# Out projection of a hybrid layer: residual loaded in place, first norm spread over the second half, four gate heads ahead, down inputs staged in residual tiles

## The chip, the cores and the metric

One core of one Trainium2 chip. The metric is the device time of one execution in microseconds. A program is timed in several runs, and their median counts; one further execution is recorded by the profiler, and its instructions are the trace.

## The reference, cut to what matters

One layer of a streaming encoder: a mixer made of two branches, a projection back to the residual stream, and a SwiGLU feed-forward network, for 1024 tokens of width 1024 in float32 (16 meta tokens stand in front and are cut off at the end).

```python
merged = jnp.sum(gates * br, axis=2)          # both branches, gated
h = h + merged @ w_out                        # out projection and residual
u = rmsnorm(h, ffn_norm_w)
gt, up = jnp.split(u @ w_gate_up, 2, axis=-1) # D_FF = 2816 each
h = h + (jax.nn.silu(gt) * up) @ w_down
return rmsnorm(h, final_norm_w)[:, N_META:]
```

The change touches the part from `merged @ w_out` to the first products of the down projection.

## The kernel before, in words

**Layout.** Activations lie transposed: 128 channels on the partitions, tokens along the free axis. Width 1024 is eight tiles (KD = 8), and the 1024 tokens fall into two halves of 512 columns, h1 and h2. Every float32 product is made of three matmuls: weights and activations are split into a rounded part (`hi`, a cast on ACT) and the remainder (`lo`, a subtraction on DVE), and hi·hi, hi·lo and lo·hi are added up in PSUM. `load_w` (L130) does this for a weight block: a load on SP into `wraw` (two buffers), the cast to `whi` on ACT (L134), the subtraction to `wlo` on DVE (L135). `split` (L145) does it for activations: cast L146, subtraction L150, or L99 where GpSimd (POOL) does it.

**Out projection (L1019 to L1067).** For each half and each of eight tiles m: load the residual slice of the input into `xr` (L1024, pool `wk`, two buffers), load the weight block, 24 matmuls, one DVE instruction that scales, adds `xr` and writes `h[m]` (L1028), a store of it to DRAM for later use (L1029), and the square summed over m (`sumsq`, L939: a square on ACT, L942 or L945, and an addition on DVE, L946). After the eighth tile `total` (L948) adds over the partitions with a matmul of ones and makes the reciprocal root: three instructions, of which the reciprocal on DVE is L186. The `wk` tiles share their addresses with the tile `part` of the stage before.

**Norm and the sums for the fast product.** Gate and up are computed together by a Strassen-like scheme: 7 products of half size per pair of blocks instead of 8. Its seven activation operands are Y11, Y21 (h1 normed), t1, t2, t3, t4 (differences) and Y22 (h2 normed). After the first half the eight tiles are normed (L1032) and split into Y11 and Y21, at once, with the subtractions in turn on DVE and POOL. After the second half two `head`s (L1002: the two products of gate block j that need only Y11 and Y21, 24 matmuls) are issued for j = 0 and 1, then 8 norms, 8 differences on DVE (L1052, L1056), 8 on POOL (L1059 for t3, L1064 for t4) and 20 splits follow. The order on each engine is made by a scheduler at build time: of what is ready by its own estimate, an engine takes what stands first in the program; on the chip each engine then works through its list in that order.

**FFN loop (L1084 to L1118).** 22 pairs j. Each needs two weight loads, weight sums on POOL (`comb`, L1081, pool `w2`, opened only after `wk` is closed), their splits (`parts`, L982 on ACT and L983 on DVE, into slots of a ring), and 84 matmuls in seven products of 12, or 60 where the head is done. The result c goes to DRAM (L1118). c and two work tiles live in `res`, a pool of 11 tiles of 128x1024; eight of these hold `h` until its last use.

**Down projection (L1121 to the end).** `h` is loaded again from DRAM into eight tiles of `res` (L1124), then for six groups of up to four c: load c into `cr` (L1134, three buffers of a pool of its own), split, 2 products per tile m, added to `h[m]` on DVE (L1144). The last group also does the squares, the final norm in three column ranges and the output.

Of the kernel before, what the change touches and what calls it, by code (L numbers as in the profile page):

```python
# [20 lines left out]
NT = 1024  # L21
# [71 lines left out]
def body(tc, A):  # L93
# [863 lines left out]
    def half(blk_, k0):  # L957
        return blk_[0][:, k0:k0 + 4], blk_[1][:, k0:k0 + 4]
# [6 lines left out]
    def bank():  # L965
        banks.append(banks.pop(0))
        return psm2(banks[-1])
# [1 line left out]
    def psm2(tag):  # L969
        return psp.tile([128, 512], F32, name="pq_" + tag, tag=tag, bufs=2 if tag in ("p", "psd") else 1)  # L970

    ring = ["whi", "wlo"]

    def slot():

        ring.append(ring.pop(0))
        t = wp.tile([128, 2, 4, 128], F32R, name="ws_" + ring[-1], tag=ring[-1], bufs=2)
        return t[:, 0], t[:, 1]

    def parts(src, w):  # L980

# [30 lines left out]
        act.activation(c[:, 0:512], ps, AF.Silu)  # L1012
        return c

    f0 = None
    a0 = a
    wkp = tc.tile_pool(name="wk", bufs=2)
    wk = wkp.__enter__()
    for hf in range(2):  # L1019
        cs = slice(512 * hf, 512 * hf + 512)  # L1020
        sm = wk.tile([128, 512], F32, name="sm")
        for m in range(KD):
            x = wk.tile([128, 512], F32, name="xr")
            sp.dma_start(x, A["hT"][:, m, NM + 512 * hf:NM + 512 * hf + 512])  # L1024
            w = load_w(A["w_out"][m])
            ps = bank()
            dense(ps, w, KD, lambda k: a[hf][0][:, k], lambda k: a[hf][1][:, k], 512)
            dve.scalar_tensor_tensor(h[m][:, cs], ps, 0.5, x, op0=ALU.mult, op1=ALU.add)  # L1028
            sp.dma_start(h_dram[:, m, cs], h[m][:, cs])  # L1029
            sumsq(wk, sm, m, cs)  # L1030
        rs = total(wk, sm, 512)
        norm = lambda k: dve.scalar_tensor_tensor(h[k][:, cs], h[k][:, cs], ffnw[:, k:k + 1], rs,  # L1032
                                                  op0=ALU.mult, op1=ALU.mult)
        fb = block(KD, 512)
        if hf == 0:
            Y["11"], Y["21"] = half(fb, 0), half(fb, 4)
            for k in range(KD):
                norm(k)
                split(fb[0][:, k], fb[1][:, k], h[k][:, cs], None if k % 2 else dve)
            continue  # L1040
        for j in range(2):
            ahead[j] = head(j)
        Y["t3"], Y["22"] = half(fb, 0), half(fb, 4)
        Y["t1"], Y["t2"], Y["t4"] = (both(room16()) for _ in range(3))
        h1, h2 = slice(0, 512), slice(512, NT)

        def put(name, k, src, eng):
            split(Y[name][0][:, k], Y[name][1][:, k], src, eng)

        for k in range(4):  # L1050
            norm(k)
            dve.tensor_tensor(h[k][:, h1], h[k][:, h2], h[k][:, h1], op=ALU.subtract)  # L1052
            put("t1", k, h[k][:, h1], dve)
        for k in range(4):
            norm(k + 4)
            dve.tensor_tensor(h[k][:, h1], h[k + 4][:, h2], h[k][:, h1], op=ALU.subtract)  # L1056
            put("t2", k, h[k][:, h1], dve)
        for k in range(4):
            pool.tensor_tensor(h[k][:, h2], h[k + 4][:, h2], h[k][:, h2], op=ALU.subtract)  # L1059
            put("t3", k, h[k][:, h2], dve)  # L1060
        for k in range(4):
            put("22", k, h[k + 4][:, h2], dve)
        for k in range(4):
# [5 lines left out]
    w2p = tc.tile_pool(name="w2", bufs=2)  # L1069
    w2 = w2p.__enter__()  # L1070
    ring[:] = ["whi", "wlo", "wr"]

    def slot3():
        ring.append(ring.pop(0))
        t = (w2 if ring[-1] == "wr" else wp).tile([128, 2, 4, 128], F32R, name="ws_" + ring[-1], tag=ring[-1],
                                                  bufs=2)
        return t[:, 0], t[:, 1]

    def comb(x, y, op):
        t = w2.tile([128, 4, 128], F32, name="sw", bufs=3)  # L1080
        pool.tensor_tensor(t, x, y, op=op)  # L1081
        return t

    for j in range(FF):  # L1084
        g = raw_w(A["w_gu"][2 * j], 0)
        u = raw_w(A["w_gu"][2 * j + 1], 1)
        x11, x12, x21, x22 = g[:, 0:4], g[:, 4:8], u[:, 0:4], u[:, 4:8]
        pc = bank()
        s1 = comb(x21, x22, ALU.add)
        if j in ahead:  # L1090
            c = ahead.pop(j)
            product(pc, parts(s1, slot3()), Y["t1"], True, True)
        else:
            c = wide()
            pa = bank()
            product(pa, parts(x11, slot3()), Y["11"], True, True)
            act.copy(c[:, 512:NT], pa)
            product(pc, parts(s1, slot3()), Y["t1"], True, True)
            product(pa, parts(x12, slot3()), Y["21"], False, True)
# [5 lines left out]
        product(pb, parts(s2, slot3()), Y["t2"], True, True)  # L1105
# [3 lines left out]
        product(pd, parts(comb(x11, x21, ALU.subtract), slot3()), Y["t3"], True, True)  # L1109
        dve.tensor_tensor(v1, u4, pd, op=ALU.add)  # L1110
        pe3 = bank()
        product(pe3, parts(comb(x12, s2, ALU.subtract), slot3()), Y["22"], True, True)
        dve.tensor_tensor(c[:, 512:NT], u4, pe3, op=ALU.add)
        act.activation(c[:, 512:NT], c[:, 512:NT], AF.Silu)
        product(pd, parts(x22, slot3()), Y["t4"], False, True)
# [3 lines left out]
    w2p.__exit__(None, None, None)  # L1119

    wk = st.enter_context(tc.tile_pool(name="wk2", bufs=2))  # L1121
    h[:] = [wide() for _ in range(KD)]
    for m in range(KD):
        sp.dma_start(h[m], h_dram[:, m])  # L1124
    for n, (q0, q1) in enumerate(DOWN):
        nq = q1 - q0
        if n % 2:
# [18 lines left out]
        if q1 < FF:  # L1146
            for m in range(KD):
                w = load_w(A["w_dn"][m, :, q0:q1], nq)
                for hf in range(2):
                    down(m, w, slice(512 * hf, 512 * hf + 512))  # L1150
        else:
            room = blk.tile([128, 2, KD, 4, 128], F32R, name="wl", tag="blk")
            ws = [load_w(A["w_dn"][m, :, q0:q1], nq, (room[:, 0, m], room[:, 1, m])) for m in range(KD)]
            for cs in (slice(0, 512), slice(512, 768), slice(768, 1024)):
                sm = wk.tile([128, 512], F32, name="sm")
                for m in range(KD):
                    down(m, ws[m], cs)
                    sumsq(wk, sm, m, cs)
                c = cs.stop - cs.start
                rs = total(wk, sm, c)  # L1160
                for k in range(KD):
                    x = h[k][:, cs]
                    if c == 512:
                        dve.scalar_tensor_tensor(x, x, finw[:, k:k + 1], rs, op0=ALU.mult, op1=ALU.mult)
                    else:
                        act.activation(x, x, AF.Copy, scale=finw[:, k:k + 1])
                        (pool if k % 3 == 1 else dve).tensor_tensor(x, x, rs, op=ALU.mult)
                    (sp, act)[k // 2 % 2].dma_start(A["out"][:, k, cs], x)
# [69 lines left out]
```

## Time and profile before

| | us |
|---|---|
| median of 3 runs | 3034.86 |
| lowest and highest run | 3029.31, 3038.34 |
| the profiled execution's own time | 3037.91 |
| its span, first to last instruction | 3036.1 |

The span is the time from the first to the last instruction of the trace. In the trace each instruction has its engine, its line, its tiles and its start and duration; matmuls are pipelined, so their durations overlap, and the spacing of their starts tells their speed. A row "A <- B" in the views of waits says that A's engine stood idle until B had ended. The granted clock of TensorE (PEclk) is given as a share of full speed.

### The profile page before, as it was taken

The page shows a single profiled execution, that of the slowest core. Times are in us where ns is not written, and L with a number is a line of the kernel's source. Part 1 is how long each engine was busy: PE and PEld are TensorE (multiplying, and loading weights), DVE is VectorE, ACT ScalarE, POOL GpSimd, SP SyncE. Part 2 cuts the span into 40 slices and gives each one's busy share as a digit, 9 for nine tenths or more (in the row PEclk, how much of TensorE's full clock was granted, in tenths as well). Part 3 has the DMA queues.
Part 4 walks back from the last instruction along what each step waited for, and adds up shares of the span by engine and source line. Part 5 has one row for each costly group of instructions (what it writes and reads, how often), then busy time and mean ns, then how long its engine had stood idle before and what let it go on. Part 6 is the DMA issues. An engine that isn't in the chain of part 4 may idle for free.

```text
span 3036.1 us, 43138 instructions
## 1 busy us (share of the span) xinstructions
PE 2921.1 (96%) x16130; PEld 2452.9 (81%) x16130; DVE 1978.2 (65%) x3846; ACT 1324.8 (44%) x3319; POOL 310.0 (10%) x286
## 2 busy tenths in 40 slices
PE   7899999999999999999999999999985999998997
PEld 6788788888888889878888778888874888886886
DVE  8577687886867854767777652564767555555446
ACT  5546465556455444645555443222233333333213
POOL 2200000000000000000010100000102333330000
PEclk9999999998999999999999999999997999999998
DMA  3121111110211211111111124352342222226312
GB/s 104 42 58 38 46 50 41 52 57 22 64 42 36 76 47 47 36 63 43 46 53 41 65 72 158 104 173 91 111 153 90 98 83 84 84 84 204 91 56 80
DMA packets 118889, 226.27 MB, mean 75 GB/s; under 512 B 46952, under 2 KB 53768, under 8 KB 118680
## 3 DMA queue, kind: packets, MB, share of 16 engines
q1 hardware_dynamic: 116952, 221.42, 22.3%
q8 instruction: 127, 2.08, 0.3%
q10 hardware_dynamic: 1728, 2.10, 0.2%
q14 instruction: 82, 0.67, 0.1%
HBM read 174.09 MB, written 49.38 MB: 74 GB/s over the span
## 4 chain that ended last, share of the span: by engine, by line
PE 83%; DVE 10%; ACT 3%; issue 2%; DMA 1%; POOL 1%; SPq 0%; DVEq 0%; ACTq 0%; POOLq 0%
PE psd L142 14%; PE psd L143 14%; PE psd L141 14%; PE pq_psd L993 1%; PE pq_p L995 1%; PE pq_psd L995 1%; PE pq_psd L994 1%; PE pq_p L993 1%; PE pq_p L994 1%; PE ps_p L561 1%; PE ps_o L639 1%; PE ps_o L746 1%; PE ps_a L617 1%; PE ps_a L629 1%; PE ps_o L619 1%
## 5 line engine op out<-in xcount | busy, mean ns | idle before, releaser
L142 PE MATMUL psd<-u_lo,whi 128*128 128x512 f32 (+3 forms) x2136 | 770.2, 361 | 3.7 <-DVE u_lo L150 2.3
L141 PE MATMUL psd<-u_hi,whi 128*128 128x512 f32 (+3 forms) x2136 | 763.8, 358 | 1.6 <-ACT raw L374 1.6
L143 PE MATMUL psd<-u_hi,wlo 128*128 128x512 f32 (+3 forms) x2136 | 757.1, 355 | 4.1 <-DVE wlo L135 4.1
L134 ACT CAST whi<-wraw 128x1024 fp32r<-128x1024 f32 (+2 forms) x197 | 188.1, 955 | 652.7 <-PE psd L142 467.7
L142 PEld LDWEIGHTS psd<-u_lo,whi 128*128 128x128 f32 x2136 | 408.4, 191 | 42.0 <-issue 6.8
L143 PEld LDWEIGHTS psd<-u_hi,wlo 128*128 128x128 f32 x2136 | 405.2, 190 | 37.2 <-DVE wlo L135 4.7
L141 PEld LDWEIGHTS psd<-u_hi,whi 128*128 128x128 f32 x2136 | 404.1, 189 | 38.0 <-issue 4.0
L135 DVE TENSOR_TENSOR wlo<-wraw,whi 128x1024 fp32r<-128x1024 f32 (+2 forms) x197 | 217.9, 1106 | 158.0 <-ACT whi L134 148.2
L143 PE MATMUL psd<-blk,wlo 128*128 128x512 f32 x512 | 199.4, 390 | 0.9 <-DVE wlo L135 0.9
L141 PE MATMUL psd<-blk,whi 128*128 128x512 f32 x512 | 199.2, 389 | 0.0
L142 PE MATMUL psd<-blk,whi 128*128 128x512 f32 x512 | 199.2, 389 | 0.0
L374 ACT COPY raw<-psd 128x256 f32<-128x256 f32 x165 | 73.4, 445 | 92.5 <-PE psd L143 89.0
L143 PEld LDWEIGHTS psd<-blk,wlo 128*128 128x128 f32 x512 | 96.1, 188 | 21.6 <-DVE wlo L135 1.8
L906 DVE TENSOR_TENSOR part<-part,psd 128x512 f32<-128x512 f32 x96 | 65.7, 684 | 72.7 <-PE psd L143 72.5
L141 PEld LDWEIGHTS psd<-blk,whi 128*128 128x128 f32 x512 | 96.1, 188 | 20.1
L142 PEld LDWEIGHTS psd<-blk,whi 128*128 128x128 f32 x512 | 96.1, 188 | 19.9
L700 DVE TENSOR_TENSOR xdt<-ps_z,dtb 128x512 f32<-128x512 f32 (+1 forms) x36 | 24.8, 690 | 105.3 <-PE ps_z L697 105.3
L1081 POOL TENSOR_TENSOR sw<-wraw 128x512 f32<-128x512 f32 x44 | 67.1, 1526 | 255.9 <-DMA wraw<-w_gu 244.8
L539 DVE TENSOR_TENSOR X<-X,itmp 66x30 f32<-66x30 f32 (+14 forms) x240 | 85.9, 358 | 5.2
L99 POOL TENSOR_TENSOR qk<-raw,qk 128x400 f32<-128x400 f32 x16 | 30.5, 1908 | 537.3 <-ACT raw L380 423.6
L537 DVE TENSOR_TENSOR itmp<-X 66x30 f32<-66x30 f32 (+14 forms) x240 | 80.8, 337 | 5.5
L421 ACT ACTIVATE Es<-ps_p,cum 128x128 f32<-128x128 f32 x256 | 75.5, 372 | 11.0 <-PE ps_p L418 10.9
(689 smaller groups left out, 6307.6 us busy)
## 6 DMA issues: line engine op xcount, KB each, us to landing
wraw<-w_in SPq DMA_DIRECT2D x105, 512.0 KB, 3.4
wraw<-w_gu SPq DMA_DIRECT2D x46, 512.0 KB, 3.4
wraw<-w_br SPq DMA_DIRECT2D x36, 512.0 KB, 3.4
c<-hc SPq DMA_DIRECT2D x22, 512.0 KB, 2.6
cr<-c SPq DMA_DIRECT2D x22, 512.0 KB, 4.1
wraw<-w_dn SPq DMA_DIRECT2D x40, 256.0 KB, 2.7
g<-zt SPq DMA_DIRECT2D x32, 256.0 KB, 2.0
y_d<-zt SPq DMA_DIRECT2D x32, 256.0 KB, 2.0
```

Of the source, the lines that this page charges most:

```text
L134: act.copy(hi[:, 0:kk], raw[:, 0:kk])
L135: dve.tensor_tensor(lo[:, 0:kk], raw[:, 0:kk], hi[:, 0:kk], op=ALU.subtract)
L141: pe.matmul(ps[:, 0:n], hi[:, wk0 + k], ahi(k), start=(k == 0), stop=False)
L142: pe.matmul(ps[:, 0:n], hi[:, wk0 + k], alo(k), start=False, stop=False)
L143: pe.matmul(ps[:, 0:n], lo[:, wk0 + k], ahi(k), start=False, stop=(k == kk - 1))
L374: dense_u((name, lambda ps, p0, p1: act.copy(raw[:, 3 + p0:3 + p1], ps)))
L421: act.activation(E[0:L, i, 0:L], ps[0:L, 128 * i:128 * i + L], AF.Relu, bias=cum[0:L, c, h0 + h:h0 + h + 1], scale=-1.0)
L537: dve.tensor_tensor(t, X[:, 0:j, j:j + 1].broadcast_to([66, j, m]), X[:, j:j + 1, j + 1:32].broadcast_to([66, j, m]), op=ALU.mult)
L539: dve.tensor_tensor(X[:, 0:j, j + 1:32], X[:, 0:j, j + 1:32], t, op=ALU.add)
L906: dve.tensor_tensor(part[:, m, cs], part[:, m, cs], ps, op=ALU.add)
L993: pe.matmul(ps, w[0][:, k], y[0][:, k], start=start and k == 0, stop=False, skip_group_check=not start)
L1081: pool.tensor_tensor(t, x, y, op=op)
```

## The change

What it does:

1. The residual slice is loaded straight into `h[m]`, and the scaled sum is added in place; the `xr` buffers go. The first half's sum of squares lies in a `res` tile.
2. The norm and the split of first-half tile m-1 are issued behind second-half tile m, one tile at a time, all on DVE.
3. Four heads (j = 0 to 3) are issued after the second half, not two.
4. The pool `w2` (third weight slot of the ring, weight sums) is opened before the out projection; heads use the ring of three.
5. The eight differences t3 and t4 move from POOL to DVE.
6. Down projection: c is loaded into `res` tiles, before `h` is reloaded and not after; `res` has 12 tiles. Pools `wk` and `wk2` have one buffer per tile, not two.

```diff
-    res = st.enter_context(tc.tile_pool(name="res", bufs=11, side="right"))
+    res = st.enter_context(tc.tile_pool(name="res", bufs=12, side="right"))
...
+    w2 = st.enter_context(tc.tile_pool(name="w2", bufs=2))
...
-    ring = ["whi", "wlo"]
+    ring = ["whi", "wlo", "wr"]
...
-    wkp = tc.tile_pool(name="wk", bufs=2)
+    wkp = tc.tile_pool(name="wk", bufs=1)
...
+    def out_tile(m, hf, cs, sm):
+        x = h[m][:, cs]
+        sp.dma_start(x, A["hT"][:, m, NM + cs.start:NM + cs.stop])
+        w = load_w(A["w_out"][m])
+        ps = bank()
+        dense(ps, w, KD, lambda k: a[hf][0][:, k], lambda k: a[hf][1][:, k], 512)
+        dve.scalar_tensor_tensor(x, ps, 0.5, x, op0=ALU.mult, op1=ALU.add)
+        sp.dma_start(h_dram[:, m, cs], h[m][:, cs])
+        sumsq(wk, sm, m, cs)
...
+    def first(k):
+        norm(k, h1, rs1)
+        put("11" if k < 4 else "21", k % 4, h[k][:, h1])
+
+    sm = wide()
+    for m in range(KD):
+        out_tile(m, 0, h1, sm)
+    rs1 = total(wk, sm, 512)
...
+    sm = wk.tile([128, 512], F32, name="sm")
+    for m in range(KD):
+        out_tile(m, 1, h2, sm)
+        if m:
+            first(m - 1)
+    first(KD - 1)
+    rs2 = total(wk, sm, 512)
+    for j in range(4):
+        ahead[j] = head(j)
...
-            pool.tensor_tensor(h[k][:, h2], h[k + 4][:, h2], h[k][:, h2], op=ALU.subtract)
-            put("t3", k, h[k][:, h2], dve)
+        dve.tensor_tensor(h[k][:, h2], h[k + 4][:, h2], h[k][:, h2], op=ALU.subtract)
+        put("t3", k, h[k][:, h2])
...
-            pool.tensor_tensor(h[k + 4][:, h1], h[k + 4][:, h1], h[k][:, h1], op=ALU.subtract)
-            put("t4", k, h[k + 4][:, h1], dve)
+        dve.tensor_tensor(h[k + 4][:, h1], h[k + 4][:, h1], h[k][:, h1], op=ALU.subtract)
+        put("t4", k, h[k + 4][:, h1])
...
-    wk = st.enter_context(tc.tile_pool(name="wk2", bufs=2))
-    h[:] = [wide() for _ in range(KD)]
-    for m in range(KD):
-        sp.dma_start(h[m], h_dram[:, m])
+    wk = st.enter_context(tc.tile_pool(name="wk2", bufs=1))
...
-            cr_ = wk.tile([128, NT], F32, name="cr", bufs=3)
+            cr_ = wide()
             sp.dma_start(cr_, c_dram[q0 + k])
...
+        if n == 0:
+            h[:] = [wide() for _ in range(KD)]
+            for m in range(KD):
+                sp.dma_start(h[m], h_dram[:, m])
...
-                sm = wk.tile([128, 512], F32, name="sm")
+                sm = wide()
```

## Rows read from the trace of the kernel before

**Rows 1.** The page's first part: TensorE's busy time.
```profile
PE 2921.1 (96%) x16130; PEld 2452.9 (81%) x16130; DVE 1978.2 (65%) x3846; ACT 1324.8 (44%) x3319; POOL 310.0 (10%) x286
```

**Rows 2.** Stretches of 10 us: PE, PEld, DVE, ACT, POOL busy (instructions), PEclk, DMA share, GB/s.
```profile
2260.00:2270.00 10.00, 10.00 (x46) 8.29 (x45) 9.47 (x9) 4.31 (x7) 1.35 (x1) 1.00 0.34 107
2270.00:2280.00 10.00, 2.68 (x12) 1.59 (x10) 10.00 (x12) 5.08 (x8) 4.99 (x3) 0.83 0.25 81
2280.00:2290.00 10.00, 10.00 (x37) 8.11 (x38) 4.08 (x5) 1.60 (x2) 0.00 (x0) 0.83 0.57 171
...
2310.00:2320.00 10.00, 9.32 (x39) 6.82 (x38) 8.05 (x10) 4.91 (x7) 0.00 (x0) 1.00 0.20 68
2320.00:2330.00 10.00, 1.01 (x5) 0.51 (x3) 9.34 (x12) 5.25 (x9) 6.20 (x3) 0.72 0.00 0
2330.00:2340.00 10.00, 0.00 (x0) 0.00 (x0) 10.00 (x8) 4.68 (x8) 9.29 (x6) 0.50 0.00 0
2340.00:2350.00 10.00, 2.93 (x6) 1.82 (x6) 10.00 (x13) 3.42 (x6) 3.98 (x3) 0.50 0.00 0
2350.00:2360.00 10.00, 8.80 (x31) 7.12 (x32) 5.02 (x8) 0.62 (x1) 3.48 (x2) 0.75 0.30 106
```

**Rows 3.** The same view, stretches of 25 us around the start of down.
```profile
2730.00:2755.00 25.00, 25.00 (x112) 20.71 (x111) 11.97 (x16) 6.68 (x11) 5.99 (x4) 1.00 0.25 83
2755.00:2780.00 25.00, 13.08 (x48) 10.01 (x47) 8.83 (x13) 5.82 (x10) 0.00 (x0) 0.73 0.81 289
```

**Rows 4.** Waits of the matmul engine, 2180 to 2500 us: total, times, longest.
```profile
PE pq_p L993 <- ACT ws_whi L982: 22.5, 1, 22.5
...
PE pq_a L143 <- DVE wlo L135: 2.8, 1, 2.8
```

**Rows 5.** Timeline of VectorE around the end of the first half: start, us, instruction.
```profile
2248.53 0.69 DVE L1028 SCALAR_TENSOR_TENSOR hc<-pq_p,xr 128x512 f32<-128x512 f32 x1 [2.71 <-PE pq_p L143]
...
2253.97 0.69 DVE L1028 SCALAR_TENSOR_TENSOR hc<-pq_z,xr 128x512 f32<-128x512 f32 x1 [2.71 <-PE pq_z L143]
...
2264.39 1.16 DVE L135 TENSOR_TENSOR wlo<-wraw,whi 128x1024 fp32r<-128x1024 f32 x1
2265.47 2.07 DVE L1032 SCALAR_TENSOR_TENSOR hc<-hc,ffnw,rs 128x512 f32<-128x512 f32 x3
...
2278.61 1.21 DVE L135 TENSOR_TENSOR wlo<-wraw,whi 128x1024 fp32r<-128x1024 f32 x1
```

**Rows 6.** Timeline of VectorE after the second half.
```profile
2316.66 1.42 DVE L1032 SCALAR_TENSOR_TENSOR hc<-hc,ffnw,rs 128x512 f32<-128x512 f32 x2
...
2332.74 1.75 DVE L150 TENSOR_TENSOR tx<-hc,tx 128x512 fp32r<-128x512 f32 x1
...
2348.06 2.48 DVE L150 TENSOR_TENSOR tx<-hc,tx 128x512 fp32r<-128x512 f32 x4
2350.47 0.68 DVE L983 TENSOR_TENSOR ws_whi<-sw,ws_whi 128x512 fp32r<-128x512 f32 x1
```

**Rows 7.** Two further stretches, columns as in rows 2.
```profile
2316.66:2350.47 33.81, 6.61 (x21) 4.19 (x20) 33.15 (x36) 15.16 (x26) 19.46 (x11) 0.61 0.00 0
...
2159.00:2216.00 57.00, 51.89 (x222) 41.35 (x221) 51.30 (x67) 18.85 (x26) 10.88 (x8) 0.99 0.43 139
```

**Rows 8.** Timeline of SyncE's DMA issues at the start of down.
```profile
2751.92 2.38 SPq L1124 DMA_DIRECT2D hc<-h_sp  x5
2763.69 0.32 SPq L1118 DMA_DIRECT2D c<-hc  x1
...
2765.92 1.52 SPq L1134 DMA_DIRECT2D cr<-c  x3
```

**Rows 9.** The same at the start of the out projection.
```profile
2215.46 0.80 SPq L1024 DMA_DIRECT2D xr<-hT  x2
```

**Rows 10.** Timeline of VectorE in the last column range of the final norm.
```profile
3022.04 0.43 DVE L946 TENSOR_TENSOR sm<-sm,sq 128x256 f32<-128x256 f32 x1 [0.41 <-ACT sq L945]
...
3022.74 0.43 DVE L946 TENSOR_TENSOR sm<-sm,sq 128x256 f32<-128x256 f32 x1
```

More of the change, by code (lines that the diff above doesn't have):

```diff
@@ L970, in psm2, with comb @@
         return psp.tile([128, 512], F32, name="pq_" + tag, tag=tag, bufs=2 if tag in ("p", "psd") else 1)
-    ring = ["whi", "wlo"]
+    ring = ["whi", "wlo", "wr"]
     def slot():
         ring.append(ring.pop(0))
-        t = wp.tile([128, 2, 4, 128], F32R, name="ws_" + ring[-1], tag=ring[-1], bufs=2)
+        t = (w2 if ring[-1] == "wr" else wp).tile([128, 2, 4, 128], F32R, name="ws_" + ring[-1], tag=ring[-1],
+                                                  bufs=2)
         return t[:, 0], t[:, 1]
+    def comb(x, y, op):
+        t = w2.tile([128, 4, 128], F32, name="sw", bufs=3)
+        pool.tensor_tensor(t, x, y, op=op)
+        return t
     def parts(src, w):
@@ L1013, in head @@
         return c
-    f0 = None
-    a0 = a
-    wkp = tc.tile_pool(name="wk", bufs=2)
+    wkp = tc.tile_pool(name="wk", bufs=1)
     wk = wkp.__enter__()
-    for hf in range(2):
-        cs = slice(512 * hf, 512 * hf + 512)
-        sm = wk.tile([128, 512], F32, name="sm")
-        for m in range(KD):
[L1023 to L1058, printed above, removed]
-            pool.tensor_tensor(h[k][:, h2], h[k + 4][:, h2], h[k][:, h2], op=ALU.subtract)
-            put("t3", k, h[k][:, h2], dve)
-        for k in range(4):
-            put("22", k, h[k + 4][:, h2], dve)
-        for k in range(4):
-            pool.tensor_tensor(h[k + 4][:, h1], h[k + 4][:, h1], h[k][:, h1], op=ALU.subtract)
-            put("t4", k, h[k + 4][:, h1], dve)
@@ L1066, in body @@
-    wkp.__exit__(None, None, None)
[L1069 to L1082, printed above, removed]
+    h1, h2 = slice(0, 512), slice(512, NT)
@@ new lines, in out_tile, with norm @@
+    def out_tile(m, hf, cs, sm):
[7 more added lines that the diff above has]
+        sumsq(wk, sm, m, cs)
+    def norm(k, cs, rs):
+        dve.scalar_tensor_tensor(h[k][:, cs], h[k][:, cs], ffnw[:, k:k + 1], rs, op0=ALU.mult, op1=ALU.mult)
@@ new lines, in put @@
+    def put(name, k, src):
+        split(Y[name][0][:, k], Y[name][1][:, k], src, dve)
+    def first(k):
[5 more added lines that the diff above has]
+    rs1 = total(wk, sm, 512)
+    fb = block(KD, 512)
+    Y["11"], Y["21"] = half(fb, 0), half(fb, 4)
+    sm = wk.tile([128, 512], F32, name="sm")
[3 more added lines that the diff above has]
+            first(m - 1)
@@ new lines, in body @@
+    first(KD - 1)
+    rs2 = total(wk, sm, 512)
+    for j in range(4):
+        ahead[j] = head(j)
+    fb = block(KD, 512)
+    Y["t3"], Y["22"] = half(fb, 0), half(fb, 4)
+    Y["t1"], Y["t2"], Y["t4"] = (both(room16()) for _ in range(3))
+    for k in range(4):
+        norm(k, h2, rs2)
+        dve.tensor_tensor(h[k][:, h1], h[k][:, h2], h[k][:, h1], op=ALU.subtract)
+        put("t1", k, h[k][:, h1])
+    for k in range(4):
+        norm(k + 4, h2, rs2)
+        dve.tensor_tensor(h[k][:, h1], h[k + 4][:, h2], h[k][:, h1], op=ALU.subtract)
+        put("t2", k, h[k][:, h1])
@@ L1084, in body @@
+    for k in range(4):
+        dve.tensor_tensor(h[k][:, h2], h[k + 4][:, h2], h[k][:, h2], op=ALU.subtract)
+        put("t3", k, h[k][:, h2])
+    for k in range(4):
+        put("22", k, h[k + 4][:, h2])
+    for k in range(4):
+        dve.tensor_tensor(h[k + 4][:, h1], h[k + 4][:, h1], h[k][:, h1], op=ALU.subtract)
+        put("t4", k, h[k + 4][:, h1])
+    wkp.__exit__(None, None, None)
     for j in range(FF):
@@ L1091, in body @@
             c = ahead.pop(j)
-            product(pc, parts(s1, slot3()), Y["t1"], True, True)
+            product(pc, parts(s1, slot()), Y["t1"], True, True)
         else:
@@ L1095, in body @@
             pa = bank()
-            product(pa, parts(x11, slot3()), Y["11"], True, True)
+            product(pa, parts(x11, slot()), Y["11"], True, True)
             act.copy(c[:, 512:NT], pa)
-            product(pc, parts(s1, slot3()), Y["t1"], True, True)
-            product(pa, parts(x12, slot3()), Y["21"], False, True)
+            product(pc, parts(s1, slot()), Y["t1"], True, True)
+            product(pa, parts(x12, slot()), Y["21"], False, True)
             act.activation(c[:, 0:512], pa, AF.Silu)
@@ L1104, in body @@
         pb = bank()
-        product(pb, parts(s2, slot3()), Y["t2"], True, True)
+        product(pb, parts(s2, slot()), Y["t2"], True, True)
         dve.tensor_tensor(u2, c[:, 512:NT], pb, op=ALU.add)
@@ L1108, in body @@
         pd = bank()
[L1109 removed]
+        product(pd, parts(comb(x11, x21, ALU.subtract), slot()), Y["t3"], True, True)
         dve.tensor_tensor(v1, u4, pd, op=ALU.add)
         pe3 = bank()
[L1112 removed]
+        product(pe3, parts(comb(x12, s2, ALU.subtract), slot()), Y["22"], True, True)
         dve.tensor_tensor(c[:, 512:NT], u4, pe3, op=ALU.add)
         act.activation(c[:, 512:NT], c[:, 512:NT], AF.Silu)
[L1115 removed]
+        product(pd, parts(x22, slot()), Y["t4"], False, True)
         dve.tensor_tensor(v0, u2, pd, op=ALU.add)
```

3 lines of the change are left out of this document (removed).

## The prediction

> **What bounds the kernel now.** I read the page's busy line first: TensorE's matmul row is busy for 96% of the span [rows 1], so no edit pays unless it fills one of the few holes in that row. Then I cut the part that the change touches into stretches of 10 and 25 us and counted matmuls in each: a stretch of 10 us at full speed shows 46, one of 25 us shows 112 [rows 2, 3]. At full speed an out tile of 24 matmuls takes 2253.97 - 2248.53 = 5.44 us, so one matmul 0.227 us [rows 5]. What is missing against that, idle time and slow clock together, is the price of a hole:
>
> - Hole B, middle of the out projection, 2270 to 2290: 12 and 37 matmuls for 46, 43 missing, 9.7 us [rows 2].
> - Hole C, after the out projection, 2310 to 2360: 39, 5, 0, 6 and 31, 149 missing, 33.8 us [rows 2].
> - Hole D, start of down, 2755 to 2780: 48 for 112, 64 missing, 14.5 us [rows 3].
> - Hole A, start of the out projection: one wait of 2.8 us on `wlo` [rows 4].
>
> Then the timelines say what ends each hole. In B the subtraction for tile 3's weights stands at 2278.61 on VectorE, behind the first half's norms and splits, which begin at 2265.47 [rows 5]. In C VectorE works from 2316.66 to 2350.47 without a pause (33.15 of 33.81 us busy, 36 instructions), and the first weight part of the FFN loop stands behind all of it, at 2350.47 [rows 6, 7]; the matmul row shows the longest wait of the stage, 22.5 us, and the clock at half (0.50) [rows 2, 4]. In D the loads of c are issued at 2765.92, behind the loads of `h` (2751.92) and behind the store of the last FFN block at 2763.69 [rows 8]. So C belongs to VectorE, D to the order on SP's queue, B to VectorE's order.
>
> **The change part by part.**
>
> *Residual in place.* Removes 16 loads into `xr` and puts 16 of the same size into `h`; instruction counts stay. The first `xr` load waits for the end of the stage before, 2215.46 [rows 9], since `wk` shares `part`'s addresses. A slice of `h` is free as soon as the previous stage has read that slice, up to 50 us earlier, so the loads move on SP's queue in between the gate and weight loads of 2159 to 2216. There they meet VectorE, which is busy for 51.30 of 57 us, and DMA engines at 0.43 [rows 7]. Hole A's `wlo` waits for VectorE, not for `xr`, so nothing is won there directly. A residual load that waits in SP's list for its slice holds the next weight load back; no row shows such a wait, so I bound it by the wait of hole A, 2.8 us [rows 4]: all of it gained, or as much again lost. I take 0.
>
> *First norm spread.* It removes nothing: 16 VectorE instructions and 8 casts as before, but tile 3's weights now stand behind two tiles of norm and split at most, and POOL's four subtractions go to VectorE. In a tile's 5.44 us VectorE has 1.2 us of weights, 0.7 each of sum and square sum and now 1.2 of norm and split, 3.8 in all, so it keeps up. What is left is the reciprocal, behind which `wlo` of tile 2 comes at 2264.39 [rows 5], just in time today. Gain between 0 (the order keeps the norms in front) and all 9.7; I take 8.5, near the whole, since 2278.61 - 2264.39 = 14.2 us between the two weight parts would be one tile's 5.44.
>
> *Four heads.* Two more heads are 48 matmuls, 10.9 us, which move from the FFN loop into hole C. They need two weight loads more in SP's list and four VectorE subtractions before or among the norms. Their operands Y11 and Y21 are finished by then.
>
> *POOL's differences to VectorE, weight sums early.* An undisturbed VectorE instruction here takes (2350.47 - 2348.06)/4 = 0.60 us; beside POOL's work one takes 1.75 [rows 6]. 36 of them would be 21.7 us, they took 33.8, so 11 POOL instructions cost VectorE 12.1, 1.1 each [rows 7]. After: 44 instructions, 26.5 us; the fourth head's two weight parts, 1.2; and three weight sums, which the early pool lets run on POOL in this stretch as three did before (three buffers), 3.3. Sum 31.0, so the loop's first weight part starts at 2347.7 and not 2350.5: 2.8 us. The heads, 21.8 us from 2308, end near 2331: TensorE then still waits some 16 us for VectorE, for in program order every split of the t operands stands ahead of the loop's weights. Together C gains 10.9 + 2.8 = 13.7; I take off 1.0 for short waits in the shorter j = 2 and 3 (no row shows them): 12.7. Lower bound 8, if half of the two heads' cover is lost to waits. Upper bound 25: the loop's first weight parts are put among the splits, and j = 0 (60 matmuls, 13.6 us) runs along with them.
>
> The Trainium skill, page "SBUF — State Buffer", section "Who interferes with whom", says that a VectorE instruction with two SBUF inputs and a GpSimd instruction that reads SBUF exclude each other for the whole instruction. By that, at the 1.7 us that POOL's instructions take here, each would cost 1.7 and not 1.1; the trace shows 1.1, and the measurement decides. By the page the eight moved differences would bring 4.8 us more and the three early sums, which it speaks against, would cost 1.8 more: C would gain 15.7.
>
> *Down inputs.* c's four loads lose their place behind eight loads of `h`; the work tiles of earlier j are free, so they can be issued where `h` is now, 2751.92, not 2765.92 [rows 8]: 14 us earlier, before the last FFN matmul. The loads of `h` go behind them; `h[0]` is first needed when tile 0's products are added. Then D ends with the casts and subtractions of the first c, which may stand behind the last FFN block's work on VectorE. I take 3 us for that, the size of hole A's wait [rows 4]. Gain 11.5. Lower bound 5, if the loads stay behind the store at 2763.69: only the issue of three and more `h` loads and their traffic goes. Upper 14.5.
>
> *One buffer per tile.* `sq` with one buffer makes a square wait for the addition before it. Under 512-column tiles there is time. In the last two ranges of the final norm the additions come every 0.70 us (3022.04, 3022.74) [rows 10]; square and addition in turn, 0.43 each and the way between, are some 0.9, so 0.2 us more for each of 14: 2.8, part of it behind other work. I take a loss of 2.0, between 0 and 4. `rs` is free when it is written again.
>
> **Sum.** A 0, B 8.5, C 12.7, D 11.5, tail -2.0: 30.7 us. The profiled execution took 3037.9, of which 1.8 lie outside its span and are not touched; after, 3007.2. It stands 3.1 above the median of the runs shown, 3034.9; against that median the forecast is 3004.2 us.
>
> **The rivals.**
>
> *Weights among the splits.* If the scheduler finds VectorE free for an instant while the splits wait for casts, the loop's weight parts go in between, C gains 25, and the time is 3004.2 - 12.3 = 2992. For it: the sums now exist early. Against: VectorE shows no pause in 33.8 us [rows 7], and it gets eight instructions more.
>
> *The c loads stay behind the last store.* D gains 5: 3004.2 + 6.5 = 3010.7. For it: SP's list is fixed, and the loads of `h` that were placed early were five, behind which the store came [rows 8]. Against: c needs four tiles only.
>
> *The norms keep their place in front of the weights.* B gains nothing: 3012.7. For it: a reciprocal that the scheduler's estimate takes as short would let norms slip ahead of weights. Against: today `wlo` of tile 2 comes right behind the reciprocal.
>
> *No change that can be told.* B and D both stay, and the single buffers and A take what C gains: 12.7 - 4 - 2.8 = 5.9 us, 3029.
>
> *Slower.* c's loads into `res` can take four of its twelve tiles as soon as c 0 to 3 are stored, in the fourth block of the loop. If they do, eight are left for c, two work tiles and the next c; a block that must wait for a store to land before it gets a tile loses the length of a product, 2.7 us, and 18 blocks lose 49 us: 3053. It decides when fewer than six tiles are free. Against: the loads of `h`, which could have been taken as early, are issued at 2751.92, at the end of the loop [rows 8].
>
> **How the numbers follow.** Forecast 3004 with a chance of 0.46; weights among the splits, 2992, 0.17; c loads late, 3011, 0.15; norms in front, 3013, 0.12; no change, 3029, 0.05; slower, 3053, 0.05. The range reaches over the first four: from 2988 (all bounds of B and D on top of 2992 leave 4 us) to 3017 (3013 and the tail at its bound of 4, A with another 2). This leaves out the last two, and some sums of mishaps. A measurement of this kernel can tell about 0.3%, 9 us, from no change: below 3026 is faster, which the first four give: 0.90. The fifth lies at 3029: same 0.05. Slower 0.05.
>
> **What would show it.** After: a stretch of 10 us behind the reciprocal in mid projection that holds 44 to 46 matmuls (B); between the last head and the first weight part of the loop one wait of 12 to 18 us, with VectorE full and the clock falling to half (C); the first c load on SP ahead of the last FFN block's store, and a wait below 4 us at the first down product (D); additions 0.9 us apart in the last column range (tail). The prediction is wrong if C's wait is gone or over 20 us, if B's wait on `wlo` still stands, or if loads into `h` hold weight loads back on SP before 2216.

## The result, and the profile after

Timed on one chip beside the kernel before, the changed kernel took 3007.87 us (median; 3007.14 to 3010.29) for 3032.09 (3028.9 to 3038.34). The ratio is 0.9916, with a 95% interval from 0.9905 to 0.9928: 0.84% less, 24 us by the medians. The forecast was 30.7 us. The profiled execution took 3007.62 us, its span 3005.8.

To see where the time went I cut both spans at the same five instructions. They are, in the timelines of POOL and VectorE (columns as in [rows 5]): the first addition of the merged branches on POOL, the eighth and the sixteenth scaled sum of the out projection, the last sum of an FFN block that reads PSUM, and the first instruction of the first square root in the last down group. The kernel before (its second cut, 2253.97, stands in [rows 5]):

```profile
2163.15 1.29 POOL L916 TENSOR_TENSOR part<-part,hc 128x512 f32<-128x512 f32 x1 [329.39 <-DVE part L912]
...
2308.16 0.69 DVE L1028 SCALAR_TENSOR_TENSOR hc<-pq_z,xr 128x512 f32<-128x512 f32 x1 [2.94 <-PE pq_z L143]
...
2761.64 0.69 DVE L1116 TENSOR_TENSOR hc<-hc,pq_psd 128x512 f32<-128x512 f32 x1 [1.43 <-PE pq_psd L995]
...
2997.26 0.69 DVE L184 TENSOR_SCALAR rs<-ps_p 128x512 f32<-128x512 f32 x1 [0.95 <-PE ps_p L950]
```

The changed kernel:

```profile
2159.45 1.28 POOL L916 TENSOR_TENSOR part<-part,hc 128x512 f32<-128x512 f32 x1 [328.95 <-DVE part L912]
...
2251.30 0.69 DVE L1032 SCALAR_TENSOR_TENSOR hc<-pq_z,hc 128x512 f32<-128x512 f32 x1 [2.75 <-PE pq_z L143]
...
2295.87 0.69 DVE L1032 SCALAR_TENSOR_TENSOR hc<-pq_z,hc 128x512 f32<-128x512 f32 x1 [2.34 <-PE pq_z L143]
...
2740.34 0.69 DVE L1115 TENSOR_TENSOR hc<-hc,pq_psd 128x512 f32<-128x512 f32 x1
...
2963.20 0.69 DVE L184 TENSOR_SCALAR rs<-ps_p 128x512 f32<-128x512 f32 x1 [0.89 <-PE ps_p L951]
```

The differences give the stretches (us); each holds one term of the forecast:

| stretch | before | after | forecast | measured |
|---|---|---|---|---|
| start to first cut (code not changed) | 2163.15 | 2159.45 | 0 | -3.7 |
| A: to the end of the first half | 90.82 | 91.85 | 0 | +1.0 |
| B: second half | 54.19 | 44.57 | -8.5 | -9.6 |
| C: norm, heads, FFN loop | 453.48 | 444.47 | -12.7 | -9.0 |
| D: down, to the last group | 235.62 | 222.86 | -11.5 | -12.8 |
| tail: to the end of the span | 38.84 | 42.60 | +2.0 | +3.8 |

The last column sums to -30.3, the difference of the spans. But -3.7 of it lies ahead of the changed code; the four changed stretches and the tail give -26.6, nearer to what the medians say.

The stretches that answer to [rows 2, 3], of the changed kernel:

```profile
2260.00:2270.00 10.00, 10.00 (x46) 8.29 (x45) 10.00 (x13) 4.12 (x7) 0.00 (x0) 1.00 0.37 123
2270.00:2280.00 10.00, 10.00 (x45) 8.28 (x45) 9.85 (x15) 4.97 (x9) 0.00 (x0) 1.00 0.48 168
...
2310.00:2320.00 10.00, 7.01 (x24) 5.36 (x23) 8.86 (x12) 5.47 (x10) 4.95 (x3) 0.83 0.00 0
2320.00:2330.00 10.00, 5.63 (x23) 3.71 (x21) 8.62 (x15) 6.86 (x13) 0.00 (x0) 0.91 0.00 0
2330.00:2340.00 10.00, 2.60 (x6) 2.13 (x7) 9.15 (x16) 2.44 (x4) 2.49 (x1) 0.50 0.01 2
2340.00:2350.00 10.00, 9.26 (x37) 7.18 (x36) 3.90 (x5) 1.75 (x3) 3.41 (x4) 0.91 0.31 105
2350.00:2360.00 10.00, 7.68 (x27) 6.24 (x28) 7.02 (x9) 2.49 (x5) 4.09 (x3) 0.83 0.35 119
...
2730.00:2755.00 25.00, 24.25 (x107) 19.73 (x106) 14.17 (x21) 6.72 (x13) 0.00 (x0) 1.00 0.80 293
```

Hole B is full: 46 and 45 matmuls. Hole D lost five matmuls of 112 (and four in the next 25 us) where it had lost 64. Hole C is smaller but there: five stretches hold 24, 23, 6, 37 and 27, 113 missing against 46 each, where 149 were missing before.

The matmul engine's waits after, 2160 to 2500 us, answer to [rows 4]; the line below "..." is the view from 2650 on:

```profile
PE pq_psd L1002 <- DVE ws_wr L990: 10.3, 1, 10.3
PE pq_a L143 <- DVE wlo L135: 3.4, 1, 3.4
PE pq_p L1000 <- DVE hc L1109: 3.1, 1, 3.1
PE pq_p L1000 <- ACT hc L1016: 3.0, 1, 3.0
...
PE pq_p L141 <- ACT blk L146: 0.7, 1, 0.7
```

The wait of 22.5 us has become 10.3, still on the loop's first weight part. Hole A's wait (3.4, it was 2.8) stayed. New is the 3.1 on line 1109, a sum that the last product of block 0 needs; it comes behind the 10.3. VectorE's timeline shows why it is late: a weight part of block 1 stands ahead of it, and VectorE waits 3.04 us for that part's cast.

```profile
2348.77 1.23 DVE L990 TENSOR_TENSOR ws_wlo<-sw,ws_wlo 128x512 fp32r<-128x512 f32 x1 [3.04 <-ACT ws_wlo L989]
...
2351.59 0.68 DVE L1109 TENSOR_TENSOR hc<-hc,pq_p 128x512 f32<-128x512 f32 x1
```

The 30 us behind the loop's first weight part, in the kernel before, in the changed one, and in the one with two heads (below), columns as in [rows 2]:

```profile
2350.47:2380.47 30.00, 28.28 (x114) 22.66 (x115) 19.38 (x26) 7.90 (x13) 14.77 (x9) 0.92 0.30 106
2336.65:2366.65 30.00, 26.20 (x99) 21.06 (x100) 19.13 (x25) 7.35 (x12) 14.68 (x9) 0.86 0.29 95
2328.34:2358.34 30.00, 27.99 (x114) 22.71 (x115) 22.10 (x29) 8.52 (x14) 11.93 (x8) 0.92 0.26 88
```

The changed kernel has 15 matmuls fewer there than the kernel before, 3.4 us. D's wait is 0.7 us.

VectorE's list in hole C, as in [rows 6]:

```profile
2305.45 1.41 DVE L1037 SCALAR_TENSOR_TENSOR hc<-hc,ffnw,rs 128x512 f32<-128x512 f32 x2
...
2336.65 0.69 DVE L990 TENSOR_TENSOR ws_wr<-sw,ws_wr 128x512 fp32r<-128x512 f32 x1
```

2336.65 - 2305.45 = 31.2 us from the first norm to the loop's first weight part; it was 33.8. SP's issues at the start of down, as in [rows 8]:

```profile
2733.97 1.85 SPq L1129 DMA_DIRECT2D hc<-c  x4
2735.86 0.97 SPq L1136 DMA_DIRECT2D hc<-h_sp  x2
2743.59 0.32 SPq L1117 DMA_DIRECT2D c<-hc  x1
```

c comes first, 9.6 us ahead of the last block's store. And SP's residual loads into `h`, the first and the last issue of 16 ([rows 9] before):

```profile
2160.76 0.33 SPq L1028 DMA_DIRECT2D hc<-hT  x1
...
2202.48 8.39 SPq L1028 DMA_DIRECT2D hc<-hT  x3
...
2212.31 2.08 SPq L133 DMA_DIRECT2D wraw<-w_out  x2
```

They run 50 us ahead. The last three take 8.4 us to issue, so SP stood waiting there, with the next weight load behind them. But that load could not have gone earlier: it is issued at 2212.31, right as the subtraction that reads its buffer ends (2211.04 + 1.21 = 2212.25, on VectorE):

```profile
2211.04 1.21 DVE L135 TENSOR_TENSOR wlo<-wraw,whi 128x1024 fp32r<-128x1024 f32 x1
```

### The profile page after: what moved, and what is told of

It is laid out like the page before. It is cut to its first block, busy times and chain, and to the rows that moved or that the text cites. A ratio compares the mean times of both kernels' runs of the same rounds, so it can differ in the third digit from the quotient of the medians.

```text
span 3005.8 us, 43124 instructions
## 1 busy us (share of the span) xinstructions
PE 2916.2 (97%) x16130; PEld 2452.7 (82%) x16130; DVE 1974.6 (66%) x3858; ACT 1324.3 (44%) x3319; POOL 289.3 (10%) x274
## 4 chain that ended last, share of the span: by engine, by line
PE 84%; DVE 9%; ACT 3%; DMA 1%; issue 1%; POOL 1%; SPq 0%; DVEq 0%; ACTq 0%; POOLq 0%
PE psd L142 15%; PE psd L143 15%; PE psd L141 15%; PE pq_p L1000 1%; PE pq_p L1001 1%; PE pq_p L1002 1%; PE ps_p L561 1%; PE ps_o L746 1%; PE pq_psd L1001 1%; PE ps_o L639 1%; PE pq_psd L1002 1%; PE pq_psd L1000 1%; PE ps_a L629 1%; PE ps_a L617 1%; PE ps_o L619 1%
```

## Experiments

All are edits of the changed kernel, but the one on the kernel before. The stretches are cut as above. "List" is the time from the second half's first norm to the first weight part of the loop; it is negative where that part comes first.

| kernel | A | B | list | C | D | tail | ratio to before (interval) |
|---|---|---|---|---|---|---|---|
| before | 90.82 | 54.19 | 33.81 | 453.48 | 235.62 | 38.84 | 1 |
| changed | 91.85 | 44.57 | 31.20 | 444.47 | 222.86 | 42.60 | 0.9916 (0.9905 to 0.9928) |
| reload of h first | 91.32 | 44.56 | 31.30 | 444.10 | 236.86 | 42.63 | 0.9953 (0.9940 to 0.9966) |
| before, c first | 91.30 | 54.22 | 33.81 | 453.30 | 221.87 | 39.07 | 0.9959 (0.9946 to 0.9971) |
| norms at once | 93.66 | 53.98 | 29.65 | 443.09 | 222.56 | 42.77 | 0.9939 (0.9927 to 0.9951) |
| differences on POOL | 90.69 | 44.56 | 34.08 | 446.01 | 221.91 | 42.70 | 0.9915 (0.9901 to 0.9929) |
| two heads | 92.51 | 44.57 | -1.08 | 446.24 | 225.18 | 42.55 | 0.9919 (0.9905 to 0.9933) |
| two heads, late sums | 93.71 | 44.59 | 30.13 | 452.82 | 221.83 | 42.62 | 0.9927 (0.9915 to 0.9940) |
| four heads, late sums | 93.26 | 44.56 | 31.93 | 444.59 | 222.17 | 42.53 | 0.9908 (0.9893 to 0.9923) |
| residual three ahead | 91.36 | 44.57 | 31.23 | 444.54 | 222.69 | 42.69 | 0.9901 (0.9887 to 0.9915) |
| two square buffers | 91.53 | 44.56 | 31.24 | 444.21 | 222.89 | 39.18 | 0.9895 (0.9881 to 0.9908) |
| block 0's weights early | 93.31 | 44.57 | 6.91 | 437.10 | 222.80 | 42.59 | 0.9893 (0.9879 to 0.9906) |
| the same, two squares | 93.37 | 44.57 | 6.91 | 437.30 | 222.33 | 39.18 | 0.9875 (0.9856 to 0.9894) |
| blocks 0 and 1, two squares | 93.54 | 44.57 | 6.91 | 431.91 | 221.85 | 39.15 | 0.9853 (0.9840 to 0.9867) |

Where an edit doesn't reach, B and the tail repeat within 0.25 us, C within 1.5 and D within 1.1 (but for D's 225.18 with two heads), while the ratios have intervals of 0.0024 to 0.0038, 7 to 12 us. So the stretches carry most of the verdicts below.

### Down: order or buffers?

The reload of `h` ahead of c again, c still in residual tiles:

```diff
+        if n == 0:
+            h[:] = [wide() for _ in range(KD)]
+            for m in range(KD):
+                sp.dma_start(h[m], h_dram[:, m])
         for k in range(nq):
             cr_ = wide()
             sp.dma_start(cr_, c_dram[q0 + k])
...
-        if n == 0:
-            h[:] = [wide() for _ in range(KD)]
-            for m in range(KD):
-                sp.dma_start(h[m], h_dram[:, m])
```

> The changed kernel with one part undone: the eight loads of h stand ahead of the first four loads of c again (c still goes to the residual tiles). Theory (the order of the loads on SP's queue made the hole at the start of down): the wait at the first down product comes back to 9 to 13 us, the stretch from the last FFN block to the last group's first square root is 10 to 14 us longer than in the changed kernel (222.9 us there), the time about 3019. Rival (the gain came from c's extra buffers in the residual tiles, not from the order): the stretch stays within 3 us and the time within 3008 to 3011.

D was 14.0 us longer, and the matmul engine's waits from 2690 us on show it again:

```profile
PE pq_p L141 <- ACT blk L146: 12.6, 1, 12.6
```

SP's timeline of this kernel has the order of [rows 8] back, c last:

```profile
2737.10 0.32 SPq L1117 DMA_DIRECT2D c<-hc  x1
2737.46 1.79 SPq L1130 DMA_DIRECT2D hc<-h_sp  x3
2739.29 2.54 SPq L1134 DMA_DIRECT2D hc<-c  x4
```

The order alone made the gain. The other direction, the kernel before with only this part (`cr_ = wide()`, the reload behind the loads of c of the first group, 11 tiles as before):

> The kernel before with one part of the change alone: c into residual tiles, loaded before h is reloaded. Theory (the parts are independent): the stretch from the last FFN block to the last group's first square root falls from 235.6 to 222 to 225 us, everything else stays, the time 10 to 14 us below the kernel before. Rival (part of that gain needs the twelfth tile or the earlier FFN end): 228 us or more.

D fell by 13.75 us to 221.87 and all other stretches stayed: median 3022.89 us, 11.9 below the kernel before beside it. The part is independent of the rest, and the twelfth tile isn't needed for it.

### Mid projection: order or POOL?

```diff
+    for k in range(KD):
+        first(k)
     for m in range(KD):
         out_tile(m, 1, h2, sm)
-        if m:
-            first(m - 1)
-    first(KD - 1)
```

> The changed kernel with the first half's eight norms and splits issued all at once ahead of the second half's tiles, all on VectorE. Theory (program order puts 16 VectorE instructions in front of the weights of tile 3): a wait on the weights' lo part of 3 to 5 us is back in mid projection, with the slow clock behind it 5 to 7 us, and the second half takes 49 to 52 us for 44.6. It is less than the 9.6 us of the kernel before, because POOL's four subtractions do not slow VectorE down here. Rival (the hole was made by POOL's subtractions beside VectorE, not by the order): no wait over 1 us, 44 to 46 us.

B went back to 53.98 us, 9.4 more, with a wait of 5.6 us on the weights of tile 3. That is more than the 49 to 52 that I expected of the order without POOL. VectorE's timeline of this kernel:

```profile
2258.83 2.06 DVE L1037 SCALAR_TENSOR_TENSOR hc<-hc,ffnw,rs 128x512 f32<-128x512 f32 x3
...
2270.74 1.22 DVE L135 TENSOR_TENSOR wlo<-wraw,whi 128x1024 fp32r<-128x1024 f32 x1
```

From the first norm to tile 3's weights are 11.9 us; they were 13.1 in [rows 5]. Four more subtractions on VectorE stand where POOL's hindrance was, and the list is only 1.2 us shorter. The hole is the order's, and the rival falls.

### Hole C: heads, sums, POOL

Two heads (`for j in range(2)`):

> The changed kernel with two heads ahead and not four. Theory (VectorE's list of norms, differences and splits sets the end of the hole, the heads only fill it): the first weight part of the FFN loop comes 1 us earlier or at the same time after the out projection, the 48 matmuls come back into the loop, and the stretch from the end of the out projection to the last FFN block is 8 to 11 us longer than in the changed kernel (444.5 us). Rival (the two extra heads delay VectorE's list by as much as they cover): under 4 us longer.

The theory was wrong: C grew by only 1.8 us, which is the rival's number. D grew by 2.3 beside a wait of 2.2 us on a cast of down weights, which the changed kernel doesn't have; what brings it is not shown. VectorE's timeline shows a list that I had ruled out:

```profile
2298.94 1.16 DVE L990 TENSOR_TENSOR ws_wlo<-sw,ws_wlo 128x512 fp32r<-128x512 f32 x1
2300.02 2.41 DVE L1037 SCALAR_TENSOR_TENSOR hc<-hc,ffnw,rs 128x512 f32<-128x512 f32 x2
```

The loop's first weight part stands ahead of the norms; the other four of block 0 stand behind the splits as before, from 2328.34 on. With two heads the two load buffers are free early, and POOL makes block 0's first sum while VectorE has the reciprocal, 5.0 us after the out projection. In the changed kernel the buffers hold heads 2 and 3: block 0's second load is issued only at 2305.56, as the last subtraction for head 3 ends, and the sum comes 13.0 us after the out projection, when the norms have begun. First the load in the changed kernel (SP), then the sum in the kernel with two heads:

```profile
2305.56 0.33 SPq L995 DMA_DIRECT2D wraw<-w_gu  x1
...
2295.64 1.29 POOL L984 TENSOR_TENSOR sw<-wraw 128x512 f32<-128x512 f32 x1 [95.60 <-DMA wraw<-w_gu]
```

The 1.8 us can be added up from counts of matmuls. From the out projection to the end of the list the kernel with two heads has 68 in 37.71 us, the changed one 104 in 40.78: two heads more but one product of block 0 less, 36 matmuls or 8.2 us won, and 3.1 lost by the longer way to the end. Another 3.4 are lost behind it (99 for 114 in 30 us, above). So the two extra heads win 8.2 us and lose 6.5 of them again, 3.1 by a later end of the list, as the rival said. Two runs take the pool away (opened behind the norms, and with it the third slot for the heads, so the two are not told apart):

```diff
-    w2 = st.enter_context(tc.tile_pool(name="w2", bufs=2))
-    ring = ["whi", "wlo", "wr"]
+    ring = ["whi", "wlo"]
...
     wkp.__exit__(None, None, None)
+    w2 = st.enter_context(tc.tile_pool(name="w2", bufs=2))
+    ring[:] = ["whi", "wlo", "wr"]
```

> Two heads ahead and the pool of the weight sums opened only after the norms, as before the change; the other parts as in the changed kernel. With two heads and the early pool, block 0's first weight part came 1.1 us before the first norm and hole C cost 446.2 us from the end of the out projection to the last FFN block. Theory (with few heads the early pool is what lets the loop's weights pass the norms): the first weight part falls back behind the splits, 26 to 32 us after the first norm, and the stretch takes 451 to 456 us. Rival (the weights passed because the load buffers were free, the pool does not matter): under 448.

> The changed kernel, four heads, with the pool of the weight sums opened only after the norms. Theory (with four heads block 0's weight parts stand behind all splits anyway, so the early pool gives nothing): the stretch from the end of the out projection to the last FFN block stays within 1.5 us of the changed kernel's 444.5 us. Rival (the early sums carry part of the gain here too): 3 us or more longer.

Both came as expected. With late sums two heads give 452.82 and four 444.59 us: the heads bring 8.2. With early sums it is 446.24 and 444.47: the heads bring 1.8. The pool brings 6.6 with two heads and 0.1 with four. In the two-head kernel with late sums VectorE's timeline has the part behind the splits again:

```profile
2302.08 1.42 DVE L1036 SCALAR_TENSOR_TENSOR hc<-hc,ffnw,rs 128x512 f32<-128x512 f32 x2
...
2332.21 0.69 DVE L989 TENSOR_TENSOR ws_whi<-sw,ws_whi 128x512 fp32r<-128x512 f32 x1
```

The differences t3 and t4 on POOL again (`dve.tensor_tensor` to `pool.tensor_tensor` in the two lines):

> The changed kernel with the eight differences t3 and t4 on POOL again. Theory (each POOL instruction costs VectorE 1.1 us, each moved instruction 0.6): VectorE's list from the first norm to the loop's first weight part is 4 us longer than in the changed kernel (31.2 us), the time 2 to 5 us longer. By the Trainium skill, page 'SBUF - State Buffer', section 'Who interferes with whom', the two engines exclude each other for the whole instruction; at 1.7 us each that would be 8.8 us longer. Rival (POOL's work runs beside VectorE's at no price): the list is 4.8 us shorter.

```profile
2305.95 1.41 DVE L1037 SCALAR_TENSOR_TENSOR hc<-hc,ffnw,rs 128x512 f32<-128x512 f32 x2
...
2340.03 0.68 DVE L990 TENSOR_TENSOR ws_wr<-sw,ws_wr 128x512 fp32r<-128x512 f32 x1
```

The list's stretch as in [rows 7], in the changed kernel and here (the counts take in an instruction or two at the edges):

```profile
2305.45:2336.65 31.20, 17.18 (x65) 12.70 (x63) 28.68 (x44) 16.25 (x29) 6.05 (x3) 0.81 0.05 17
2305.95:2340.03 34.08, 17.75 (x65) 12.69 (x63) 32.94 (x38) 16.55 (x30) 18.93 (x11) 0.79 0.05 15
```

The list took 34.08 us, 2.9 more where 4 were expected. It has seven VectorE instructions of 0.60 us fewer (36 for 43; in the changed kernel the last split comes behind the weight part), so each POOL instruction cost the list (2.9 + 4.2)/8 = 0.89 us. VectorE also stood idle less, 1.1 us for 2.5; by its busy time, 32.94 for 28.68, the price is (4.26 + 4.2)/8 = 1.06 us. Of the 2.9 us, 1.5 reached C, no more than C varies; the ratio can't tell it. The Trainium skill, page "SBUF — State Buffer", sections "SBUF: two separate sides" and "Who interferes with whom", says that of two such instructions the one that starts first holds the ports for its whole length and the other is blocked. By that, as an estimate at 1.7 us each, the list would be 8.8 us longer; the trace shows a subtraction beside POOL at 1.75 us [rows 6] but not that sum, and the measurement decides. The 1.7 us seem to hold waiting of POOL's own: beside the reciprocal its sum took 1.29 (2295.64, above).

### What was left of hole C

Block 0's weight sums and splits written ahead of the norms (`loop_w` holds its loads, `comb` and `parts`), its products left where they were:

```diff
+    early = {0: loop_w(0)}
     for k in range(4):
         norm(k, h2, rs2)
...
+        if j in early:
+            p1, p2, p3, p4, p5 = early.pop(j)
```

> The changed kernel with the weight sums and weight splits of FFN block 0 written ahead of the second half's norms, so that they stand in front of the splits of the t operands in program order. Theory (what is left of the hole is only the place of block 0's weight parts behind all of the activation splits): the wait of 10.3 us is split into waits under 4 us, block 0 runs along with the splits, and the stretch from the end of the out projection to the last FFN block is 8 to 13 us shorter than in the changed kernel (444.5 us), the time about 2998. Rival (VectorE's amount of work, not its order, sets the end: Y22 and t4 come last anyway): under 4 us shorter.

C fell by 7.4 us to 437.10. The wait of 10.3 us is gone; the longest now is

```profile
PE pq_psd L1002 <- DVE ws_wlo L990: 4.4, 1, 4.4
```

block 1's weights, next in VectorE's list. The theory holds; the 7.4 us lie just under the 8 to 13 expected, and block 0's first part comes 6.9 us after the first norm, not 31.2. With block 1 as well (`early = {0: loop_w(0), 1: loop_w(1)}`), and two square buffers:

> Weight parts of FFN blocks 0 and 1 ahead of the norms, and two square buffers. Theory (what is left after block 0's weights went ahead is block 1's, one wait of 4.4 us): the stretch from the end of the out projection to the last FFN block is 2 to 5 us shorter than with block 0 alone (437.3 us). Rival (the two load buffers and the six weight slots hold block 1 back, and its parts block VectorE's list): the same or longer.

C fell to 431.91, another 5.4 us, just over the 2 to 5 expected. In its view of waits the 4.4 us is gone; after the wait of hole A the longest are 2.7 us (on ACT's copy in a head) and 2.6 (on the cast of a weight part). Its median is 2991.35 us, and its ratio to the kernel before (0.9840 to 0.9867) lies wholly below the changed kernel's (0.9905 to 0.9928): this version beats both.

### Tail and residual

Two buffers for the squares of the final norm (`name="sq", bufs=2`):

> The changed kernel with two buffers for the squares of the final norm again, and nothing else. Theory (the one buffer makes square and addition take turns): the additions of the last column range come 0.7 us apart and not 0.91, the stretch from the first square root of the last group to the end is 2 to 4 us shorter than in the changed kernel (42.6 us). Rival (the tail is longer for another reason, such as the place of the squares behind the output's issues on ACT): under 1 us shorter.

The changed kernel's additions in the last column range, from VectorE's timeline as in [rows 10]:

```profile
2990.97 0.43 DVE L947 TENSOR_TENSOR hc<-hc,sq 128x256 f32<-128x256 f32 x1 [0.48 <-ACT sq L946]
2991.88 0.43 DVE L947 TENSOR_TENSOR hc<-hc,sq 128x256 f32<-128x256 f32 x1 [0.48 <-ACT sq L946]
```

0.91 us apart. With two buffers:

```profile
2987.77 0.42 DVE L947 TENSOR_TENSOR hc<-hc,sq 128x256 f32<-128x256 f32 x1
2988.47 0.43 DVE L947 TENSOR_TENSOR hc<-hc,sq 128x256 f32<-128x256 f32 x1 [0.28 <-ACT sq L946]
```

0.70, and the tail is 39.18 us, 3.4 shorter. Together with block 0's early weights:

> Both edits together: block 0's weight parts ahead of the norms and two square buffers. If they are independent, the gains add up: 10 to 17 us below the changed kernel, 2991 to 2998. If the earlier end of the FFN loop runs into a later limit (loads of c, the output's issues), less than the sum.

C 437.30 and tail 39.18: the gains add up by stretch (the median, 2999.73, is above what I expected, with the earlier stretches at their longer end).

The residual in spare tiles (`x = wide()[:, 0:512]`, three free):

> The changed kernel with the residual slices loaded into spare residual tiles, three ahead at most, and not in place. Theory (16 loads hoisted in among the gate loads cost the stage before 1 us of waits): the stretch from that stage's first POOL addition to the end of the first half is 0 to 2 us shorter than 91.9 us, the rest is the same. Rival (loading in place is what makes the start of the out projection no worse): 2 us or more longer.

A was 91.36, 0.5 less. But A lies between 90.69 and 93.71 over all kernels, 11 of which load the residual in the same way, as the changed one does. A difference of 1 us can't be read from that; what the loads in place cost or bring stays open, below 3 us.

## Why the prediction was right, and where it was not

**B, right.** -8.5 forecast, -9.6 measured. The step named the order, and undoing the order alone brought the hole back. The residue of 1.2 us that I kept did not come: 46 and 45 matmuls in the stretches, though VectorE has nothing to spare in them (10.00 and 9.85 of 10 us busy).

**D, right, a little low.** -11.5 forecast, -12.8, and -13.75 alone. I kept 3 us for the casts and subtractions of the first c behind the last block; the wait was 0.7. The rival with c behind the store did not come: four c loads were placed before it, two of `h` after them.

**C, right in sign, too large by 3.7.** From the out projection to the loop's first weight part the kernel before had 56 matmuls in 42.31 us; the changed kernel has 104 in 40.78. So all 48 matmuls of the two heads found room, 10.9 us as forecast. The end came 1.5 us earlier and not 2.8, since the fourth head's two weight parts stand before the norms and the list begins 9.58 us after the projection where it was 8.50.

The list itself, 31.0 us forecast and 31.2 measured, was right partly by luck. The sum held 44 instructions and the fourth head's parts, 1.2 us; the list has 43 and not those parts. In their place VectorE stood idle 2.5 us, waiting for casts, where I had counted on no pause. TensorE's wait is 10.3 us, under the 12 to 18 that I gave as the sign, because its work ahead of the wait lasted 31 us from the out projection and not 23, with a wait of 3.0 us on ACT in a head and the slow clock behind it. That cost nothing, as the list sets the end.

The term that failed is the 1.0 us taken off for short waits in j = 2 and 3. The loss was 3.4 us and lay in block 0: block 0's last weight parts came at the end of VectorE's list, the two load buffers came free late, block 1's weights with them, and VectorE waited for block 1's cast with line 1109 behind it, which held TensorE for 3.1 us with the slow clock after it. The sum is then 10.9 + 1.5 - 3.4 = 9.0.

The reason that I gave, that in program order every split stands ahead of the loop's weights, is only half of what decides. It holds for the changed kernel: written ahead of the norms, block 0's first part comes 6.9 us after the first norm and not 31.2. But with two heads one part was ready before any norm was, and it went first although it stands later in the program. That heads 2 and 3 hold the load buffers and so make block 0 late is read from the timeline; no run gives four heads more buffers. So 10.9 us is not what the two extra heads are worth: in C it is 1.8 beside the early pool and 8.2 without it. The rival "weights among the splits" was real, but for fewer heads or with the weights written first, and for block 0 alone it was worth 7.4 us, not 12.3.

**POOL.** 1.1 us for each instruction from [rows 7] stands against 1.06 by busy time and 0.89 by the list from the run.

**The third sign.** I had said that the prediction is wrong if loads into `h` hold weight loads back on SP before 2216. SP did wait 8.4 us with the last three, but the weight load behind them was waiting for its own buffer until 2212.25, so it lost nothing. In the view of SP's waits from 2150 to 2250 us, 15 waits of weight loads end with such a subtraction and one with a sum of squares, none with a residual load.

**Tail, low.** +2.0 forecast, +3.8 measured, 3.4 of it the square buffer. In the last range the spacing was as forecast (0.9). In the range before it the additions come 1.00 us apart (2976.72, 2977.72) and with two buffers 0.67 (2975.82, 2976.49), so 0.2 us for each of 14 was too little, and little of it was hidden.

**A.** 0 forecast, +1.0 measured, within what A varies.

**The sum.** 30.7 forecast for the profiled executions and 30.3 measured, but 3.7 of that came from code in front of the change, which is luck. Errors in C and in the tail of 3.7 and 1.8 us were partly made up by B and D, 2.4. Against the medians the gain was 24 us. The measured 3007.87 lies 3.7 us over the forecast of 3004.2, inside its range; but that forecast started from 3034.9, and the kernel before took 3032.09 beside the changed one, so in gain the miss is 6.5 us.

## What to carry to other kernels

Where a list scheduler fills each engine, ask of each late instruction what makes it ready, buffers above all: more work ahead that takes the load buffers can leave the next stage's first weights behind a long list, and writing those weights earlier in the program brought more (12.6 us with two blocks) than the work ahead itself. Order loads by who waits for them: four loads in front of eight were worth 13 us. Count a buffer in the last stage as if nothing hid its wait.

## What the runs showed that I had not expected

The spread of the total is made in code that none of these kernels changes. The first addition on POOL of the stage before the out projection, the first cut above, began between 2153.5 and 2163.2 us in the fourteen profiled executions, 9.6 us apart, more than most edits here are worth, while B, free of edits, repeats within 0.03 us. The granted clock in 700 to 725 us divides the fourteen without overlap: it is 1.00 in the five that begin between 2153.5 and 2155.3, 0.80 in the five between 2159.4 and 2161.2, and 0.66 in the four between 2161.9 and 2163.2. The stretch of 710 to 720 in the kernel before, at half the clock, and in the last kernel of the table, at the full clock (columns as in [rows 2]):

```profile
710.00:720.00 10.00, 10.00 (x50) 8.04 (x49) 3.57 (x13) 4.30 (x18) 0.00 (x0) 0.50 0.00 0
710.00:720.00 10.00, 10.00 (x77) 8.25 (x76) 5.32 (x18) 6.51 (x29) 0.00 (x0) 1.00 0.00 0
```

TensorE is busy throughout in both. The kernel before was profiled at 0.66 and the changed one at 0.80, which goes with the -3.7 us of the result. Why the clock falls in some executions and not in others is not shown. A comparison of stretches between the same instructions tells a gain of 3 us that the ratio can't tell.
